# Hyena filters kept in two parts, and the side pieces of the sums over k1 placed elsewhere

## The chip, the core and the metric

The kernel runs on one core of a Trainium2 chip. TensorE (PE) multiplies matrices, its weight loads (PEld) run beside them; VectorE (DVE), ScalarE (ACT) and GpSimd (POOL) do elementwise work; SyncE (SP) issues DMAs, and so do ACT and POOL from their own instruction queues. The metric is the device time of one execution in microseconds (us), less is better. The kernel before takes 3728.32 us, the median of 3 runs (3725.71 to 3728.37).

## What is computed

One encoder block in float32. The change touches the Hyena branch alone, a gated long convolution applied twice, whose filters come from a small network over the positions:

```python
filt = (hid @ w_out).reshape(l, HYENA_ORDER, 2, HYENA_WIDTH)
filt = filt * jnp.exp(-t[:, None] * deltas[None, :])[:, None, None, :]   # decay
kern = jnp.concatenate([filt[:, :, 0], zeros, filt[:0:-1, :, 1]], axis=0)
spec = jnp.fft.rfft(kern, axis=0)                                        # L = 2048, CW = 512 channels

def long_conv(z, spec):
    zf = jnp.fft.rfft(z, n=2 * l, axis=1)
    return jnp.fft.irfft(zf * spec[None], n=2 * l, axis=1)[:, :l]

for n in range(2):                                  # the two orders
    z = gates[n] * (long_conv(z, spec[:, n]) + skip[n] * z)
```

## The kernel before

Every float32 product is made of two-part operands: `split` (L40 to L43) writes hi, a rounded copy, on ACT and lo, the rest, on DVE; `mm3` (L46 to L50) is three matmuls: hi hi, hi lo, lo hi. In the trace L42 and L43 are such splits, and L48 to L50 the three matmuls.

The stages follow each other: the projections (to about 690 us), attention (to about 1510), the Hyena branch (to about 2095), the merge (to about 2600) and the experts. All engines work through fixed queues; a scheduler sets each queue's order ahead of the run from the order of the code.

**The filters.** `filter_gen` (L629) runs as a side piece of the projections, one step beside one group of their matmuls, from about 315 to 592 us. For 4 blocks of channels, 2 orders and 4 pieces of positions it makes two tiles `fo` (128x512): two matmuls each (L654), a product with the decay `dc` on DVE (L656), and two stores of 128 KB on SP's queue (`store_l1`) into the scratch array `filt`.

**The Hyena branch.** `hyena_phase` (L669) transforms in two steps, n = n1, n2 and k = k1, k2, in four rounds: two orders, two halves of the channels. A round has three transforms forward: the two filters (`spectrum` with s = 0 and s = 1) and the data (`conv`). Each begins with `first`, the sums over n1: 8 pieces of 128x512, for each 12 matmuls of 256 columns against `d1` (so 96 in all) and two splits of the sums into `bh` (ACT) and `bl` (DVE). The sums over n2 follow, for the filters 132 matmuls of the table `tf` in 9 steps. `conv` makes its sums over n2, multiplies with the spectrum (`ya`, cut by ACT into `yh` and by POOL into `yl`) and sums back over k2 with tables `tg`, in 17 steps (`back`: ACT takes the result out as `vo` and stores it in `s_v`). `last` then sums over k1: 16 tiles `vr` are read back from `s_v`, split into `vh` and `vl`, multiplied with `d3` (6 matmuls a tile), scaled with the skip and gated (`z`, `g`).

`last` is a generator of 36 steps, and it runs as the side piece of the round that follows: `next(side)` takes a step. In the kernel before, `first` takes one at every second piece, `spectrum` 14 over its 9 steps (9, and 5 more at every k0 that divides by 4), and what is left is drained ahead of `conv`. In the first round the side piece is the rest of the gate projection (matmuls `gp` with tiles `gu`) and a step is taken at every piece.

**The pieces.** `parts_of` (L723) reads filters and data alike: SP loads a raw piece `zr` of 256 KB (L731), in 512-byte runs, up to 3 ahead; `split_pool` (L719) cuts it into `zh` on ACT (L720) and `zl` on POOL (L721).

Of the kernel before, what the change touches and what calls it, by code (L numbers as in the profile page):

```python
# [19 lines left out]
L = 2048  # L20
# [73 lines left out]
def proj_phase(E, x, norm1_g, w_in, conv_w, conv_b, qg, kg, rope, qn, kn, vs, hyc, ud, sg, mlp, gen):  # L94
# [6 lines left out]
    with ExitStack() as ctx:  # L101
# [76 lines left out]
        with pool_of(tc, name="pj_q", bufs=2) as pq:  # L178
            with pool_of(tc, name="pj_x", bufs=4) as px, pool_of(tc, name="pj_pt", bufs=3, space=PSUM) as pt:
                turn(0, px, pt)  # L180
                w = weights(0)
                gq = pc.tile([128, 2, DK], F32, name="gq")
                nc.sync.dma_start(gq[:, 0], dap(qg, 0, [[0, 128], [1, DK]]))
                nc.sync.dma_start(gq[:, 1], dap(kg, 0, [[0, 128], [1, DK]]))
                rp = pc.tile([128, NT, 2, 16], F32, name="rp")
# [443 lines left out]
def filter_gen(E, w, tabs, hsd, filt):  # L629

    nc, tc = E.nc, E.tc
    with pool_of(tc, name="fl_o", bufs=2, side="right") as po, pool_of(tc, name="fg_ps", bufs=2, space=PSUM) as ps:
        for ct in range(4):
            for o in range(2):
                wo = po.tile([128, 2, 128], F32, name="wo", bufs=1)
                for s in range(2):
                    nc.sync.dma_start(wo[s * 64:(s + 1) * 64], w["w_out"][0].rearrange("h (o s c) -> h o s c", o=2, s=2)
                                      [:, o, :, ct * 128:(ct + 1) * 128])
                weo = po.tile([128, 2, 128], F32, name="weo", bufs=1)
                nc.vector.tensor_tensor(weo[:, 0], wo[:, 0], wo[:, 1], ALU.add)  # L640
                nc.vector.tensor_tensor(weo[:, 1], wo[:, 0], wo[:, 1], ALU.subtract)
                wh = po.tile([128, 2, 128], F32R, name="woh")
                wl = po.tile([128, 2, 128], F32R, name="wol")
                split(nc, wh, wl, weo)
                for i in range(4):
                    dc = po.tile([128, 512], F32, name="dc")
                    nc.sync.dma_start(dc, tabs["decay"][ct * 128:(ct + 1) * 128, i * 512:(i + 1) * 512])
                    hs = po.tile([128, 512], F32R, name="hs")
                    nc.gpsimd.dma_start(hs, hsd[:, i * 512:(i + 1) * 512])
                    fs = []  # L650
                    for s in range(2):
                        p = ps.tile([128, 512], F32, name="fq")
                        for a, ww in enumerate((wh, wl)):
                            nc.tensor.matmul(p, ww[:, s], hs, start=a == 0, stop=a == 1)  # L654
# [3 lines left out]
                        if s == 0:  # L658
                            yield
                    if i == 0:  # L660
                        c = po.tile([128, 1], F32, name="c0")
                        nc.vector.tensor_tensor(c, fs[0][:, 0:1], fs[1][:, 0:1], ALU.add)
                        nc.vector.tensor_scalar(fs[0][:, 0:1], c, 0.5, None, ALU.mult)
                    for s in range(2):
                        store_l1(nc.sync, filt, (o * 2 + s) * CW * L, ct, i, fs[s])
                    yield


def hyena_phase(E, hyc, filt, skip, tabs, scr, hT, filler, then):  # L669
# [7 lines left out]
    with pool_of(tc, name="hy_d", bufs=1) as pd, ExitStack() as right:  # L677
        with ExitStack() as ctx:
# [21 lines left out]
            with pool_of(tc, name="hy_e", bufs=1) as pe:  # L700
                ex = pe.tile([8, 128], F32, name="ex")
                nc.sync.dma_start(ex, tabs["ex"])
                sk = pe.tile([8, 2, 64], F32, name="sk")
                for o in range(2):
                    nc.sync.dma_start(sk[:, o], dap(skip, o * CW, [[64, 8], [1, 64]]))
                skb = pd.tile([128, 2, 64], F32, name="skb")
                p = s1.tile([128, 128], F32, name="p1")
                nc.tensor.matmul(p, ex, sk.rearrange("p o g -> p (o g)"), start=True, stop=True)
                nc.scalar.activation(skb, p.rearrange("p (o g) -> p o g", o=2), AF.Copy)
# [13 lines left out]
            def parts_of(jobs):  # L723

                todo = [(src, hf * 8 + q) for src, hf in jobs for q in range(8)]
                loads, ready = [], []

                def load():
                    src, q = todo.pop(0)
                    r = p1.tile([128, 4, 128], F32, name="zr", bufs=AHEAD)  # L730
                    nc.sync.dma_start(r, dap(src, q * 512, [[8192, 128], [128, 4], [1, 128]]))  # L731
                    loads.append(r)

                def cut():
                    r = loads.pop(0)
                    zh = p1.tile([128, 4, 128], F32R, name="zh", bufs=CUT[0])
                    zl = p1.tile([128, 4, 128], F32R, name="zl", bufs=CUT[0])
                    split_pool(zh, zl, r)
                    ready.append((zh, zl))
                    if todo:  # L740
                        load()
# [3 lines left out]
                cut()  # L745
                while ready:
                    while loads and len(ready) < CUT[0]:
                        cut()
                    yield ready.pop(0)

            AHEAD, CUT = 3, [2]

            def first(it, v, side, busy=False):
# [3 lines left out]
                for q in range(8):  # L757
# [10 lines left out]
                    if busy or q % 2:  # L768
                        next(side, None)
# [969 lines left out]
```

## Time and profile before

| what | value |
| --- | --- |
| median of 3 runs | 3728.32 us (3725.71 to 3728.37) |
| profiled execution, its own time | 3731.11 us |
| its span, first to last instruction | 3729.3 us |
| mean granted TensorE clock | 0.987 |
| PE busy | 3608.1 us, 97% |
| DVE busy | 2472.5 us, 66% |
| ACT busy | 1819.2 us, 49% |
| POOL busy | 412.9 us, 11% |
| DMA | 607.28 MB, mean 163 GB/s |

Busy shares are means over stages with different limits. A stretch of the trace is read by its length, the matmuls that PE has in it, and what ended PE's waits. Matmuls of one chain overlap: the time from one start to the next, the pitch, is what a matmul costs, and it is less than its duration.

### The profile page before, as it was taken

To read this page: it belongs to the slowest core of one execution; us is meant where nothing else is said; L and a number is where in the kernel's file an instruction comes from. 1 tells how busy PE (TensorE), PEld (TensorE's weight loads), DVE (VectorE), ACT (ScalarE), POOL (GpSimd) and SP (SyncE) were. 2 spreads that over 40 slices of the span, in tenths; PEclk is the share of its full clock that TensorE was granted. 3 is DMA by queue.
4 is the path that set the end of the run, shared out by engine and by line. 5 is a ranking of instruction groups with operands and counts; after the bars stand their busy time and mean duration, and the time that the engine had idled before them with its cause. 6 is when DMAs were issued, how large, how long until landed. Compare 5 with 4: busy or idle time off the path is not lost. (4 is left out here: it accounts for less than half of the span.)

```text
span 3729.3 us, 55700 instructions
## 1 busy us (share of the span) xinstructions
PE 3608.1 (97%) x21122; PEld 3117.1 (84%) x21122; DVE 2472.5 (66%) x5459; ACT 1819.2 (49%) x2787; POOL 412.9 (11%) x423
## 2 busy tenths in 40 slices
PE   8999999999999999999999799998999999999998
PEld 6788888788888888788998678887998888888887
DVE  8944552598989898256787754548875666665663
ACT  5411111566676666357667533323445555555553
POOL 0000000000000000344553200000000101101000
PEclk9999999999999999999999899998999999999999
DMA  4286774322222231757776853324666766766664
GB/s 157 75 246 170 193 187 135 119 64 68 96 81 94 68 102 60 227 165 227 210 214 192 286 170 130 115 91 138 216 194 204 222 206 208 221 203 210 220 204 123
DMA packets 449713, 607.28 MB, mean 163 GB/s; under 512 B 37467, under 2 KB 333411, under 8 KB 442789
## 3 DMA queue, kind: packets, MB, share of 16 engines
q1 hardware_dynamic: 388149, 436.71, 37.1%
q0 software_dynamic: 34736, 127.16, 12.7%
q10 hardware_dynamic: 26560, 39.85, 3.0%
q8 instruction: 166, 2.72, 0.3%
q14 instruction: 102, 0.84, 0.1%
HBM read 464.16 MB, written 139.46 MB: 162 GB/s over the span
## 5 line engine op out<-in xcount | busy, mean ns | idle before, releaser
L43 DVE TENSOR_TENSOR wl<-r,wh 128x2048 fp32r<-128x2048 f32 (+1 forms) x248 | 476.9, 1928 | 333.1 <-ACT wh L42 333.0
L42 ACT ACTIVATE wh<-r 128x2048 fp32r<-128x2048 f32 (+1 forms) x248 | 402.5, 1624 | 383.6 <-PE pg L1616 138.4
L1616 PE MATMUL pg<-x,wh 128*128 128x512 f32 x1664 | 587.0, 398 | 0.0
L1619 PE MATMUL pg<-x,wl 128*128 128x256 f32 x1664 | 466.3, 280 | 0.0
L1616 PEld LDWEIGHTS pg<-x,wh 128*128 128x128 f32 x1664 | 312.4, 188 | 75.3
L411 DVE TENSOR_SCALAR_CACHE_REDUCE x<-p 128x512 f32<-128x512 f32 x512 | 335.0, 685 | 22.8 <-PE p L410 22.0
L410 PE MATMUL p<-k,qT 128*128 128x512 f32 x1024 | 327.3, 415 | 0.0
L1619 PEld LDWEIGHTS pg<-x,wl 128*128 128x128 f32 x1664 | 314.1, 189 | 0.5
L418 ACT ACTIVATE x<-x,sm 128x2048 f32<-128x2048 f32 x128 | 256.7, 2005 | 45.8 <-DVE sm L415 42.0
L42 ACT ACTIVATE ah<-pt 128x512 fp32r<-128x512 f32 x256 | 150.2, 595 | 151.9 <-PE pt L433 151.3
L48 PE MATMUL p<-wh,uh 128*128 128x512 f32 x512 | 203.5, 398 | 0.4 <-ACT uh L134 0.4
L49 PE MATMUL py<-wl,hh 128*128 128x512 f32 x512 | 203.3, 397 | 0.0
L48 PE MATMUL py<-wh,hh 128*128 128x512 f32 x512 | 201.8, 394 | 0.0
L43 DVE TENSOR_TENSOR bl<-p,bh 128x512 fp32r<-128x512 f32 x192 | 124.6, 685 | 115.5 <-ACT bh L42 114.7
L49 PE MATMUL p<-wl,uh 128*128 128x512 f32 x512 | 200.5, 392 | 0.4 <-DVE wl L43 0.4
L50 PE MATMUL py<-wh,hl 128*128 128x512 f32 x512 | 200.5, 392 | 0.0
L43 DVE TENSOR_TENSOR al<-pt,ah 128x512 fp32r<-128x512 f32 x256 | 174.9, 686 | 38.5 <-ACT ah L42 37.5
L50 PE MATMUL p<-wh,ul 128*128 128x512 f32 x512 | 200.4, 392 | 0.0
L410 PEld LDWEIGHTS p<-k,qT 128*128 128x128 f32 x1024 | 171.3, 189 | 24.4 <-ACT qT L368 2.8
L433 PE MATMUL pt<-idf,x 128*128 128x128 f32 x1024 | 164.7, 272 | 0.0
L48 PE MATMUL gp<-gh,gu 128*128 128x512 f32 x384 | 158.3, 412 | 4.1 <-ACT go L294 3.4
L1642 POOL DMA_INDIRECT out_dram<-y,ix x32 | 67.8, 2118 | 808.0 <-ACT y L1641 698.3
(433 smaller groups left out, 9346.8 us busy)
## 6 DMA issues: line engine op xcount, KB each, us to landing
r<-in_w_gate SPq DMA_DIRECT2D x64, 1024.0 KB, 5.2
r<-in_w_up SPq DMA_DIRECT2D x64, 1024.0 KB, 5.8
r<-in_w_down SPq DMA_DIRECT2D x64, 1024.0 KB, 5.8
gu<-s_ud POOLq DMA_DIRECT2D x48, 1024.0 KB, 5.9
tg<-in_tg POOLq DMA_DIRECT2D x68, 384.0 KB, 4.2
xt<-in_x SPq DMA_DIRECT2D x32, 512.0 KB, 4.3
s_filt<-fo SPq DMA_DIRECT2D x128, 128.0 KB, 3.2
zr<-s_filt SPq DMA_DIRECT2D x64, 256.0 KB, 3.1
```

The lines of the kernel that those rows point to most:

```text
L42: nc.scalar.activation(hi, src, AF.Copy)
L43: return nc.vector.tensor_tensor(lo, src, hi.bitcast(F32), ALU.subtract)
L48: nc.tensor.matmul(out, a[0], b[0], start=start, stop=False)
L49: nc.tensor.matmul(out, a[0], b[1], start=False, stop=False)
L50: return nc.tensor.matmul(out, a[1], b[0], start=False, stop=stop)
L410: nc.tensor.matmul(p, qT[:, t * 2 + m, a], k2[:, m, o:o + 512], start=a == 0, stop=a == 1)
L411: nc.vector.tensor_scalar(x[:, o:o + 512], p, 0.125, None, ALU.mult, ALU.max, accum_out=sm[:, c * 2 + i:c * 2 + i + 1])
L418: nc.scalar.activation(x, x, AF.Exp, bias=sm[:, 8 + m:9 + m], accum_out=acc)
L433: nc.tensor.transpose(p[:, i, t * 128:(t + 1) * 128], EX[u, t, 0][:, (g * 2 + i) * 128:(g * 2 + i + 1) * 128], E.idf)
L1616: nc.tensor.matmul(p.rearrange("p a c -> p (a c)"), wt[0][:, k, cs], x2[:, k].rearrange("p a c -> p (a c)"), start=k == 0, stop=False, ski ...
L1619: nc.tensor.matmul(p[:, 0], wt[1][:, k, cs], x2[:, k, 0], start=False, stop=k == KD - 1, skip_group_check=True)
L1642: nc.gpsimd.indirect_dma_start(out=rows, out_offset=bass.IndirectOffsetOnAxis(ap=ix[:, s:s + 1], axis=0), in_=y, in_offset=None, compute_o ...
```

## The change

`filter_gen` now cuts each tile itself: ACT writes hi and DVE writes lo, side by side in a tile of 128x4x2x128, and `keep` stores both, two DMAs of 256 KB a tile in runs of 1 KB. The scratch array is twice as large. The loops over orders and pieces change places, so that `dc` and `hs` are loaded once for both orders (16 times each, and not 32). The factors from `w_out` take the buffers of `dc`, and two small constants move between pools (left out below).

`parts_of` reads a filter piece ready cut, hi and lo in one DMA of 512 KB, now from POOL's queue, into 4 buffers; a data piece is still raw, read by SP and cut by ACT and POOL. The load of piece n + 4 is issued after piece n is used.

The side steps: `first` takes one at its sixth piece and five behind its last; `spectrum` takes 9 and one more; `conv` takes 6 in `first` and drains the rest behind it.

```diff
         for ct in range(4):
-            for o in range(2):
...
-                for i in range(4):
...
+            ww = [factors(ct, o) for o in range(2)]
+            for i in range(4):
+                dc = po.tile([128, 4, 128], F32, name="dc")
...
+                for o in range(2):
                     fs = []
                     for s in range(2):
                         p = ps.tile([128, 512], F32, name="fq")
...
-                        f = po.tile([128, 512], F32, name="fo")
-                        nc.vector.tensor_tensor(f, p, dc, ALU.mult)
+                        f = po.tile([128, 4, 2, 128], F32R, name="fo")
+                        nc.vector.tensor_tensor(f[:, :, 1].bitcast(F32), p.rearrange("p (a b) -> p a b", b=128), dc,
+                                                ALU.mult)
...
+        def keep(f, o, s, ct, i):
+            raw = f[:, :, 1].bitcast(F32)
+            split(nc, f[:, :, 0], f[:, :, 1], raw)
+            for h in range(2):
+                nc.sync.dma_start(dap(filt, (o * 2 + s) * CW * L * 2 + ((ct * 2 + h) * 16 + i * 4) * 16384,
+                                      [[256, 64], [16384, 4], [1, 256]]),
+                                  f[h * 64:(h + 1) * 64].rearrange("p a b c -> p a (b c)").bitcast(F32))
...
                 def load():
-                    src, q = todo.pop(0)
-                    r = p1.tile([128, 4, 128], F32, name="zr", bufs=AHEAD)
-                    nc.sync.dma_start(r, dap(src, q * 512, [[8192, 128], [128, 4], [1, 128]]))
-                    loads.append(r)
+                    src, q, two = todo.pop(0)
+                    z = p1.tile([128, 4, 2, 128], F32R, name="zz", bufs=AHEAD)
+                    r = None
+                    if two:
+                        nc.gpsimd.dma_start(z.rearrange("p a b c -> p (a b c)"),
+                                            dap(src, q * 1024, [[16384, 128], [1, 1024]]))
+                    else:
+                        r = px.tile([128, 4, 128], F32, name=("ya", "vo")[q % 2], bufs=2)
+                        nc.sync.dma_start(r, dap(src, q * 512, [[8192, 128], [128, 4], [1, 128]]))
+                    loads.append((z, r))
...
                         split(nc, hi, lo, p.rearrange("p g k c -> p k g c"))
-                    if busy or q % 2:
+                    if busy or q == 5:
+                        next(side, None)
+                if not busy:
+                    for _ in range(5):
                         next(side, None)
                 return B
...
-                    if not busy and k0 % 4 == 0:
+                    if not busy and k0 == 8:
                         next(side, None)
...
-                B = first(it, 0, side)
+                B = first(it, 0, side, False)
+                for _ in side:
+                    pass
...
-                    for _ in side:
-                        pass
                     conv(it, hf, side)
```

ACT's queue at the first piece sums of a later round (s = 0, the stretch from 1696.7 to 1708.0 us in the trace of before). `zh` is the cut of a piece, `bh` the first part of the sums over n1, `vh` of a tile read back for the sums over k1, `sp` the spectrum. Before:

```order
L720 ACTIVATE zh<-zr 128x512
L42 ACTIVATE vh<-vr 128x512
L42 ACTIVATE bh<-p_16965 128x32x16
L42 ACTIVATE bh<-p_16974 128x32x16
L720 ACTIVATE zh<-zr 128x512
L42 ACTIVATE bh<-p_16989 128x32x16
L42 ACTIVATE bh<-p_16998 128x32x16
L42 ACTIVATE vh<-vr 128x512
```

The same place after:

```order
L42 ACTIVATE bh<-p_16872 128x32x16
L42 ACTIVATE bh<-p_16881 128x32x16
L42 ACTIVATE vh<-vr 128x512
L42 ACTIVATE bh<-p_16898 128x32x16
L42 ACTIVATE bh<-p_16907 128x32x16
L42 ACTIVATE vh<-vr 128x512
L42 ACTIVATE bh<-p_16918 128x32x16
L42 ACTIVATE bh<-p_16927 128x32x16
L42 ACTIVATE vh<-vr 128x512
```

The cuts `zh` are gone from this place; the first `vh` still stands ahead of the last copies of the sums, four here and two before.

ACT's queue at the second filter of the same round (s = 1, 1725.1 to 1739.3 us before). `z` is the scaling with the skip. Before:

```order
L42 ACTIVATE bh<-p_17311 128x32x16
L720 ACTIVATE zh<-zr 128x512
L42 ACTIVATE bh<-p_17332 128x32x16
L42 ACTIVATE bh<-p_17341 128x32x16
L720 ACTIVATE zh<-zr 128x512
L42 ACTIVATE bh<-p_17356 128x32x16
L42 ACTIVATE bh<-p_17365 128x32x16
L720 ACTIVATE zh<-zr 128x512
L42 ACTIVATE vh<-vr 128x512
```

After, where `zz<-ya` and `zz<-vo` are cuts of the data pieces that follow:

```order
L42 ACTIVATE bh<-p_17257 128x32x16
L918 ACTIVATE z<-z,skb 128x128
L42 ACTIVATE bh<-p_17268 128x32x16
L918 ACTIVATE z<-z,skb 128x128
L42 ACTIVATE bh<-p_17277 128x32x16
L739 ACTIVATE zz<-ya 128x4x128
L42 ACTIVATE bh<-p_17289 128x32x16
L42 ACTIVATE bh<-p_17298 128x32x16
L739 ACTIVATE zz<-vo 128x4x128
```

Between two copies of the sums there stands now a cut for the data or a scaling, and no longer the cut that the next matmuls of this stretch need.

POOL's queue at the end of a round, where `conv` runs out and the next round's filter pieces come. Before:

```order
L832 DMA tg<-in_tg 128x768
L721 TENSOR_TENSOR yl<-ya,yh 128x512
L832 DMA tg<-in_tg 128x768 x2
L721 TENSOR_TENSOR yl<-ya,yh 128x512
L721 TENSOR_TENSOR zl<-zr,zh 128x512
L832 DMA tg<-in_tg 128x768
```

After:

```order
L740 TENSOR_TENSOR yl<-ya,yh 128x512
L753 DMA zz<-s_filt 128x1024
L860 DMA tg<-in_tg 128x768
L740 TENSOR_TENSOR yl<-ya,yh 128x512
L753 DMA zz<-s_filt 128x1024
L860 DMA tg<-in_tg 128x768
L753 DMA zz<-s_filt 128x1024 x5
```

Loads of filter pieces, each of which waits for PE to free its buffer, now stand in this queue ahead of the last `yl` of the round.

## Rows read from the trace of the kernel before

**Rows 1.** Waits, 1525 to 2095 us: waiting engine, line, cause: us, times, longest.

```profile
PE p L48 <- DVE bl L43: 14.0, 10, 2.3
...
PE p L50 <- POOL yl L721: 2.9, 8, 0.5
...
ACT vh L42 <- DMA vr<-s_v: 15.9, 13, 2.6
```

**Rows 2.** Windows: length, busy (count) of PE, PEld, DVE, ACT, POOL; clock, DMA share, GB/s.

```profile
1533.30:1555.50 22.20, 19.65 (x126) 16.93 (x125) 10.59 (x16) 14.18 (x26) 16.16 (x17) 1.00 0.88 277
1604.80:1615.70 10.90, 8.36 (x62) 7.35 (x60) 5.87 (x9) 8.61 (x19) 6.03 (x7) 1.00 0.97 293
1725.10:1739.30 14.20, 13.06 (x104) 12.45 (x103) 12.46 (x22) 13.35 (x29) 8.38 (x7) 1.00 0.71 220
1858.00:1872.70 14.70, 13.49 (x105) 12.60 (x104) 12.39 (x22) 13.52 (x29) 8.40 (x7) 1.00 0.77 223
1987.50:2003.90 16.40, 14.20 (x104) 13.74 (x104) 13.33 (x23) 14.06 (x30) 9.05 (x7) 0.91 0.74 227
1627.80:1641.90 14.10, 13.02 (x107) 12.61 (x105) 9.54 (x15) 12.45 (x25) 8.75 (x7) 1.00 0.34 96
...
2021.40:2035.50 14.10, 11.96 (x97) 11.55 (x96) 10.88 (x21) 11.85 (x24) 6.47 (x5) 1.00 0.38 132
1696.70:1708.00 11.30, 8.99 (x70) 8.35 (x68) 7.34 (x12) 9.46 (x19) 7.65 (x8) 0.97 0.70 215
...
1739.30:1760.50 21.20, 18.76 (x146) 17.61 (x145) 10.58 (x22) 12.65 (x31) 2.48 (x3) 1.00 0.70 228
...
2003.90:2021.40 17.50, 17.50 (x147) 17.50 (x146) 9.72 (x21) 12.84 (x30) 1.84 (x2) 0.99 0.74 239
...
1800.00:1810.00 10.00, 10.00 (x86) 10.00 (x85) 8.69 (x20) 5.53 (x12) 7.08 (x8) 1.00 0.82 215
2000.00:2010.00 10.00, 10.00 (x74) 10.00 (x73) 6.61 (x13) 8.53 (x20) 3.64 (x5) 0.83 0.83 269
...
1520.00:1530.00 10.00, 7.61 (x27) 5.83 (x26) 0.00 (x0) 0.60 (x1) 4.58 (x9) 0.83 1.12 356
540.00:560.00 20.00, 20.00 (x89) 16.47 (x88) 8.71 (x16) 2.41 (x4) 1.06 (x2) 1.00 0.66 164
```

**Rows 3.** Groups by form, 1525 to 2095 us: busy, mean ns of one, idle before.

```profile
L43 DVE TENSOR_TENSOR bl<-p,bh 128x512 fp32r<-128x512 f32 x192 | 124.6, 685 | 115.5 <-ACT bh L42 114.7
...
L720 ACT ACTIVATE zh<-zr 128x512 fp32r<-128x512 f32 x96 | 61.1, 637 | 13.2 <-DMA zr<-s_filt 8.5 <-DMA zr<-s_hyc 2.0 <-DMA zr<-s_z 1.7
```

**Rows 4.** Timeline of PE, ACT, DVE, POOL: start, us, instruction, idle before it and cause.

```profile
1706.81 0.38 PE L48 MATMUL p<-vh,d 128*128 128x256 f32 x1 [2.31 <-DVE bl L43]
...
1999.66 0.39 PE L48 MATMUL p<-d,zh 128*128 128x256 f32 x1 [2.10 <-DVE bl L43]
...
1696.89 0.60 ACT L815 ACTIVATE vo<-p 128x512 f32<-128x512 f32 x1 [0.58 <-PE p L50]
...
1704.80 0.63 ACT L42 ACTIVATE vh<-vr 128x512 fp32r<-128x512 f32 x1 [0.61 <-DMA vr<-s_v]
1705.34 1.07 ACT L42 ACTIVATE bh<-p 128x512 fp32r<-128x512 f32 x2
...
1706.07 2.66 DVE L43 TENSOR_TENSOR bl<-p,bh 128x512 fp32r<-128x512 f32 x4
...
1697.16 0.55 POOL L832 DMA_DIRECT2D tg<-in_tg  x1
```

**Rows 5.** DMA issues of the whole run: queue, count, KB each, median us to landing.

```profile
tg<-in_tg POOLq DMA_DIRECT2D x68, 384.0 KB, 4.2
xt<-in_x SPq DMA_DIRECT2D x32, 512.0 KB, 4.3
```

**Rows 6.** Tile `fo`: what DVE, idle, waited for before it: us, times.

```profile
  DMA dc<-in_decay: 10.0, 4
  DMA s_filt<-fo: 4.5, 2
```

More of the change, by code (lines that the diff above doesn't have):

```diff
@@ new lines, in factors @@
+        def factors(ct, o):
+            wo = po.tile([128, 4, 128], F32, name="dc")
+            for s in range(2):
+                nc.sync.dma_start(wo[s * 64:(s + 1) * 64, :2],
+                                  w["w_out"][0].rearrange("h (o s c) -> h o s c", o=2, s=2)
+                                  [:, o, :, ct * 128:(ct + 1) * 128])
+            nc.vector.tensor_tensor(wo[:, 2], wo[:, 0], wo[:, 1], ALU.add)
+            nc.vector.tensor_tensor(wo[:, 3], wo[:, 0], wo[:, 1], ALU.subtract)
+            wh = po.tile([128, 2, 128], F32R, name="woh")
+            wl = po.tile([128, 2, 128], F32R, name="wol")
+            split(nc, wh, wl, wo[:, 2:])
+            return wh, wl
@@ new lines, in keep @@
+        def keep(f, o, s, ct, i):
[5 more added lines that the diff above has]
+                                  f[h * 64:(h + 1) * 64].rearrange("p a b c -> p a (b c)").bitcast(F32))
+        for ct in range(4):
+            ww = [factors(ct, o) for o in range(2)]
+            for i in range(4):
+                dc = po.tile([128, 4, 128], F32, name="dc")
+                nc.sync.dma_start(dc.rearrange("p a b -> p (a b)"),
+                                  tabs["decay"][ct * 128:(ct + 1) * 128, i * 512:(i + 1) * 512])
+                hs = po.tile([128, 512], F32R, name="hs")
+                nc.gpsimd.dma_start(hs, hsd[:, i * 512:(i + 1) * 512])
+                for o in range(2):
@@ L699, in hyena_phase @@
             nc.gpsimd.dma_start(d3, tabs["d3"])
[L700 to L709, printed above, removed]
+            AHEAD = 4
+            e2 = p1.tile([8, 2, 128], F32, name="zz", bufs=AHEAD)
+            nc.sync.dma_start(e2[:, 0], tabs["ex"])
+            for o in range(2):
+                nc.sync.dma_start(e2[:, 1, o * 64:(o + 1) * 64], dap(skip, o * CW, [[64, 8], [1, 64]]))
+            skb = pd.tile([128, 2, 64], F32, name="skb")
+            p = s1.tile([128, 128], F32, name="p1")
+            nc.tensor.matmul(p, e2[:, 0], e2[:, 1], start=True, stop=True)
+            nc.scalar.activation(skb, p.rearrange("p (o g) -> p o g", o=2), AF.Copy)
             TF = {}
@@ L723, in parts_of @@
             def parts_of(jobs):
-                todo = [(src, hf * 8 + q) for src, hf in jobs for q in range(8)]
+                todo = [(src, hf * 8 + q, two) for src, hf, two in jobs for q in range(8)]
                 loads, ready = [], []
                 def load():
-                    src, q = todo.pop(0)
-                    r = p1.tile([128, 4, 128], F32, name="zr", bufs=AHEAD)
-                    nc.sync.dma_start(r, dap(src, q * 512, [[8192, 128], [128, 4], [1, 128]]))
-                    loads.append(r)
@@ L740, in cut @@
+                    loads.append((z, r))
+                def cut():
+                    z, r = loads.pop(0)
+                    if r is not None:
+                        split_pool(z[:, :, 0], z[:, :, 1], r)
+                    ready.append(z)
+                while todo and len(loads) < AHEAD:
+                    load()
+                while loads:
+                    while loads and len(ready) < 3:
+                        cut()
+                    yield ready.pop(0)
                     if todo:
@@ L741, in cut, with first @@
                         load()
-                while todo and len(loads) < AHEAD:
-                    load()
[L745 to L753, printed above, removed]
+                yield from ready
+            def first(it, v, side, busy):
                 B = (pb.tile([128, KR, 256], F32R, name="bh"), pb.tile([128, KR, 256], F32R, name="bl"))
@@ L757, in first @@
                 for q in range(8):
-                    zh, zl = next(it)
+                    z = next(it)
                     for a in range(2):
```

47 lines of the change are left out of this document (15 added, 32 removed).

## The prediction

> **What bounds the kernel now.** I read the busy shares first: PE is busy for 97% of the span, so a change pays only where PE stands still or runs slower, and of the rest nothing is worth a look unless PE waits for it. The waits of PE inside the Hyena branch come next [rows 1]: the largest is for `bl`, the second part of the sums over n1 (14.0 us in 10 waits); those for `yl` are small, 2.9 us. The first part feeds it: DVE sat idle for 115.5 us ahead of the `bl`, nearly all of it waiting for ACT's `bh` [rows 3]. So ACT sets the pace of the sums over n1.
>
> Windows of the branch by stage then give a loss for each stretch: its length less its matmuls times their pitch. PE never stands still from 1800 to 1810 us and starts 86 matmuls of 256 columns there, so the pitch is 10/86 = 0.116 us; from 540 to 560 it starts 89, mostly of 512 columns, which makes 0.225 us [rows 2]. A piece is 12 matmuls, 1.40 us of PE. For it ACT makes two `bh`, started 1.07 us a pair [rows 4], and, before the change, one `zh` of 0.64 us [rows 3]; consecutive ACT copies start about 0.1 us sooner than their durations add up to, so a piece costs ACT about 1.6 us, more than PE's 1.40, with the `vh` and `z` of the side piece on top. DVE's `bl`, four in 2.66 us [rows 4], need 1.33 us a piece: they just fit.
>
> The losses so found [rows 2]: the four sums over n1 of s = 1 lose 3.7 (10.9 us with 62 matmuls), 2.1 (14.2 with 104), 2.5 (14.7 with 105) and 4.3 (16.4 with 104), together 12.6 us. The first stretch of the branch loses 22.2 - 96 x 0.116 - 30 x 0.225 = 4.3. Those of s = 0 lose 11.3 - 70 x 0.116 = 3.2 in the one shown; two others are alike (11.5 and 11.2 us long). The four data stretches lose between 1.0 and 2.8; the first and the last are shown (1.7 and 2.8), and the sum is 6.7. The sums over n2 behind s = 1 lose 4.2 in the one from 1739.3 and 0.4 in the one from 2003.9; 1.2 lies between.
>
> There is a second loss. The window from 2000 to 2010 us has PE busy throughout, but 74 matmuls and not 86, at a granted clock of 0.83 [rows 2]; it begins with a pause of 2.10 us that ended at 1999.66 [rows 4]. The clock has two levels here, 2.4 and 1.2 GHz, and 0.83 over 10 us is 3.4 us at the lower one: 0.17 x 10 = 1.7 us lost. The pause of 2.31 us before 1706.81 [rows 4] is followed by the same.
>
> **Part by part.** Gains are negative.
>
> *First stretch, filter pieces ready cut.* ACT loses 8 `zh` and POOL 8 `zl` that PE's first 96 matmuls waited for. What can go is the loss of 4.3. What can come are waits for loads twice as large, on POOL's queue among the tables for the sums over n2, in a stretch that already moves 277 GB/s [rows 2]: 2 MB more at the highest rate shown, 356 GB/s, are 5.9 us, of which the loads issued ahead of the stretch hide some. Bounds -4.3 and +4; I take -3, near the lower, as PE's own work of 18 us leaves 2.2 us for each of the 8 loads.
>
> *Sums over n1 of s = 1.* ACT loses 8 `zh` a stretch and takes 4 cuts of the data instead, of the same 0.64 us; most of the `vh` move behind the sums. The order shows `bh` pairs with one cut or one short `z` between. That is 8 x 1.07 + 4 x 0.54 + some z and vh, about 13 us beside PE's 12.2: nearly balanced, and what is late is off PE's path, since the cuts are for the next stretch. What is late next are the loads. A piece's load is issued when the fourth before it is used, 3 x 1.40 = 4.2 us ahead of its need, and POOL's issue itself takes 0.55 [rows 4]. By size it lies between `tg` (384 KB, 4.2 us) and anything larger; `xt`, of the same 512 KB, took 4.3 us [rows 5]. So the first late piece slips by about 0.6 us, later ones by 0.1 to 0.2 each: 1.0 us a stretch, and 0.3 for the rest. The first of the four I leave 1.4 us more of its 3.7, since the tables of the first round are still being loaded beside it (293 GB/s). -12.6 + 4 x 1.3 + 1.4 = **-6.0**. Bounds: -11 if loads and copies both keep up, +7 by the first rival.
>
> A rule of the Trainium skill bears on this term and can be left out of it: the page "DMA: Bandwidth & Descriptors", section "Anatomy of one DMA — SWDGE (gpsimd) path", fits the time of a DMA from POOL's queue as 2.0 us plus its bytes over 436 thousand per us. By it `tg` would land after 2.9 us, where the trace has 4.2, so the measurement decides here; with the page's 3.2 us for 512 KB the loads would never slip, and the sum would be lower by 4 x 1.0 us.
>
> *The clock behind 2003.9.* The pause of 2.10 us is one of ACT's and goes with it: **-1.7** (0 if it stays above 2 us).
>
> *Sums over n2 of s = 1.* They took 14 side steps and take 10, with fewer copies between ACT's `sp`: of 5.8 us lost I take **-2.3**; bounds 0 and -4.5.
>
> *Data stretches.* The first four pieces are cut ahead of the stretch, during s = 1, and the side pieces stand behind the sums, where the copies of the last `bl` would have made PE wait: the `d3` matmuls fill that. Of 6.7 us **-3**; bounds 0 and -5. The loads are as large as before.
>
> *Sums over n1 of s = 0, rounds 2 to 4.* Here the end is set by another chain: the last `back` of the round before is done at 1696.89, ACT's `vo` is stored, SP reads `vr` back, and ACT's `vh` starts at 1704.80, having waited for that read [rows 4] (such waits are 15.9 us over the branch [rows 1]). The changed order keeps that `vh` in ACT's queue, now ahead of four `bh` of this stretch and not two. Behind it DVE has two `vl` and five `bl`, some 4.7 us, to do before the sums over n2 can begin; before it had one `vl` and four `bl` (3.3 us). So the stretch grows by about 1.4 us less the 0.2 that the `zh` cost: **+1.2 x 3 = +3.6**, and the pause of 2.3 us with its slower clock stays. Bounds: -6 (a read that lands by the time its turn comes leaves only PE's work) and +6.
>
> *The last `yl` of a round.* On POOL's queue it stands behind a load that waits until PE has used the first piece of the next round (12 matmuls, 1.4 us); PE's last `back` needs that `yl`. Hitherto each of these waits was 0.5 us at most [rows 1]. About 1.2 us of stall, less 0.5 that PE can fill with sums over n1 that are ready: 0.7 x 3 = **+2**; bounds 0 and +4. Behind the load queue also a `tg`, which has two steps of slack.
>
> *Projections.* 64 tiles are cut, each 0.6 us of ACT and 0.69 of DVE. Between 315 and 592 us PE does not wait for the filters: in the 20 us shown it is at 20.00 while DVE has 8.71 and ACT 2.41 [rows 2]. The two stores of a tile grow from 128 to 256 KB on SP's queue and the ring `fo` has two buffers; DVE waited 4.5 us for it and 10.0 for `dc` [rows 6], and of `dc` half the loads go. Cover is PE's queue of matmuls that need neither. **+1**; bounds 0 and +8, the latter if a late `fq` stops PE's queue at a change of weights, with four such tiles ahead of it.
>
> **Sum.** -3 - 6.0 - 1.7 - 2.3 - 3 + 3.6 + 2 + 1 = -9.4 us. The profiled execution took 3731.1 and would take 3721.7. It lies 2.8 us above the median of the three timed runs, which therefore goes from 3728.3 to **3719**.
>
> **Rivals.** *Loads become the bound (slower).* Filter pieces ask for 524 KB each 1.40 us, 375 GB/s, and the highest that the branch shows is 356 GB/s, with the DMA engines' share above 1 [rows 2]. The other traffic in the s = 1 stretch from 1987.5 is 227 GB/s x 16.4 us less 8 x 262 KB, so 99 GB/s, which leaves 257, or 2.04 us a piece. Three pieces at 0.64 and the first 0.6 make 2.5 us a stretch, over 8 stretches 20 us, of which 7.6 stand in the sum: +12.4. Pauses of that size would bring the lower clock to four stretches, +6.8: **3738**. It decides from about 2 us a stretch. Against it: much of that other traffic are reads for the side piece, which moves behind the sums, and a read of 4 KB runs asks for fewer packets than one of 512 bytes. Chance 0.15.
>
> In a sentence by itself: the Trainium skill, "Trainium Kernel Development and Optimization", section "Key Constraints", says that DMAs from SP, ACT and POOL run on the same 16 DMA engines and interleave, so that moving the filter loads to POOL's queue gives them no bandwidth of their own; no row here contradicts it.
>
> *The pauses move and stay.* The sums over n2 wait behind the side pieces for the same `bl` and `vl`; only the first stretch, the data and half of s = 1 gain: -3 - 3 - 3 + 3.6 + 2 + 1 = -2.4, **3726**, no measurable change. For it speaks that DVE needs 1.33 of 1.40 us a piece [rows 4], which five side steps add to. Chance 0.22.
>
> *More than that.* The stretch from 2021.4 loses 2.8 us in shorter pauses at a granted clock of 1.00 [rows 2]; only the pauses above 2 us have the slower clock behind them. If the five side steps behind the sums fill those, three more dips of 1.7 go, s = 0 costs nothing instead of 3.6, and the loads slip by 0.3: -5.1 - 3.6 - 2.8 = -11.5 beyond the forecast, **3707.5**. Chance 0.15.
>
> *Projections stall* at +8 instead of +1: **3726**. Chance 0.06. The forecast itself, 3712 to 3726, keeps 0.42.
>
> **Chances and range.** A measurement tells about 0.2% from no change, 7.5 us: faster is below 3720.9, slower above 3735.8. The forecast lies on that line's faster side by 2 us, so it gives 0.25 to faster and 0.17 to same; the second rival 0.04 and 0.18, the third 0.15 to faster, the first 0.15 to slower, the last 0.05 to same and 0.01 to slower. Faster 0.44, same 0.40, slower 0.16. The range runs from 3702, below the third rival's time, to 3738, the first's.
>
> **What would show it.** Right: s = 1 stretches of about 13 us with no `zh` on ACT and waits of PE for `zz` loads near 1 us; s = 0 stretches near 12.5 us ended by `vh` waiting for `vr`; PE at 10.00 in the projections' windows. Wrong: waits of PE for `zz` above 2 us a stretch (first rival), long waits for `bl` still behind s = 1 (second), a granted clock of 1.00 behind every sum over n1 (third), PE idle between 315 and 620 us (fourth).

## The result, and the profile after

The changed kernel takes 3779.37 us (median of 4 runs, 3776.23 to 3785.95) against 3728.35 us beside it: a ratio of 1.0132, with a 95% interval of 1.0119 to 1.0144. It is 51 us slower where I forecast 9 us less. Its profiled execution has a span of 3780.4 us at a mean clock of 0.983.

Two markers place the loss. The first weight load of the gate projection `gp` ends the projections, the first of the merge, `pb`, ends the Hyena branch. The rows are those of tiles `gp` and `hi`, with first and last start; before comes first, after second.

```profile
L48 PEld LDWEIGHTS gp<-gh,gu x384: 186/188/333, 687.7 to 1603.9; 128*128 128x128 f32 x192
L48 PEld LDWEIGHTS pb<-wah,hi x128: 186/188/333, 2095.1 to 2496.0; 128*128 128x128 f32 x128
```

```profile
L48 PEld LDWEIGHTS gp<-gh,gu x384: 186/188/333, 707.9 to 1625.6; 128*128 128x128 f32 x192
L48 PEld LDWEIGHTS pb<-wah,hi x128: 186/188/334, 2147.9 to 2546.3; 128*128 128x128 f32 x128
```

The projections end 20.2 us later. From there to the merge it was 1407.4 us and is 1440.0: 32.6 more. Attention lies in that stretch; up to the branch's first sums over n1 it took 845.6 us and takes 847.5. What follows the merge's start is 1.7 us shorter. So there are two losses, in two stages, of which the sum had +1 and about -10.

PE's waits in the branch, 1500 to 2150 us, answer [rows 1]: engine, line, cause, us in total, times, longest.

```profile
PE p L48 <- DVE bl L43: 21.5, 12, 4.8
PE p L48 <- DMA zz<-s_filt: 20.6, 13, 7.2
PE p L48 <- ACT vo L843: 9.3, 8, 3.8
...
PE p L50 <- POOL yl L740: 2.5, 4, 0.7
```

The waits for `bl`, which the change was to remove, grew from 14.0 to 21.5; a new one for filter pieces, 20.6 us, stands beside them. In the projections PE waited for nothing of the sort before. Now, 250 to 700 us:

```profile
PE fq L670 <- DVE fo L672: 6.0, 4, 2.3
PE p L48 <- ACT wh L42: 5.6, 3, 3.4
```

Windows of the changed kernel (columns as in [rows 2]): first the projections where the loss lies, then the three s = 0 stretches of rounds 2 to 4.

```profile
510.00:520.00 10.00, 5.33 (x13) 2.76 (x12) 5.10 (x8) 2.41 (x4) 0.53 (x1) 0.70 0.70 185
520.00:530.00 10.00, 6.93 (x26) 4.67 (x25) 3.03 (x5) 1.78 (x3) 0.00 (x0) 0.96 0.78 224
530.00:540.00 10.00, 7.83 (x23) 6.20 (x24) 7.85 (x16) 4.72 (x9) 0.53 (x1) 0.66 0.85 242
...
630.00:640.00 10.00, 8.09 (x28) 6.07 (x27) 0.92 (x3) 4.30 (x6) 2.13 (x3) 0.83 0.51 172
```

```profile
1722.40:1739.00 16.60, 10.19 (x78) 9.26 (x76) 7.79 (x12) 8.35 (x15) 4.23 (x8) 1.00 1.12 392
1860.60:1879.60 19.00, 11.53 (x80) 10.78 (x79) 8.77 (x15) 8.15 (x15) 3.92 (x8) 0.90 1.01 348
2000.20:2019.80 19.60, 12.02 (x81) 10.88 (x80) 8.87 (x15) 8.14 (x15) 4.23 (x8) 0.90 1.00 340
```

**The projections.** From 510 to 540 us PE starts 62 matmuls where 136 fit, and from 630 to 640 28 of 46: 92 matmuls of 0.225 us, 20.7 us, the whole loss. The waits named there are some 11.6 us; the granted clock of 0.66 and 0.70 shows the rest, PE at the lower level after pauses of 2.2 to 3.4 us. Both places are boundaries between blocks of weights. SP's queue around the first, with start, time and instruction:

```profile
515.49 4.65 SPq L653 DMA_DIRECT2D s_filt<-fo  x4
520.18 0.80 SPq L143 DMA_DIRECT2D r<-in_w_in  x1
521.81 5.32 SPq L653 DMA_DIRECT2D s_filt<-fo  x4
527.18 0.79 SPq L143 DMA_DIRECT2D r<-in_w_in  x1
```

The next block's weights `r` stand between groups of four filter stores, and each group waits until its tiles are cut. PE meanwhile waits for the products and then for the weights:

```profile
514.08 0.79 PE L670 MATMUL fq<-hs,woh 128*128 128x512 f32 x1 [2.31 <-DVE fo L672]
...
532.17 0.80 PE L48 MATMUL p<-uh,wh 128*128 128x512 f32 x1 [3.42 <-ACT wh L42]
```

**The branch.** From the first matmul over n1 behind the last `back` to the first over n2, the s = 0 stretches of rounds 2 to 4 grew from 11.3, 11.5 and 11.2 us to 16.7, 19.0 and 19.6: 21.3 us of the 32.6. In them PE now waits 7.0 us for pieces, where it waited for none, and 14.5 us for `bl`, where it was 6.9. The DMA engines were busy for 0.70 to 0.80 there at 215 to 245 GB/s, and now for all the time at 340 to 392. Round 3 on ACT, SP and PE:

```profile
1862.05 0.60 ACT L843 ACTIVATE vo<-p 128x512 f32<-128x512 f32 x1 [1.96 <-DMA s_v<-vo]
1862.68 0.37 ACTq L848 DMA_DIRECT2D s_v<-vo  x1
...
1874.89 0.63 ACT L42 ACTIVATE vh<-vr 128x512 fp32r<-128x512 f32 x1 [6.29 <-DMA vr<-s_v]
```

```profile
1869.62 0.88 SPq L894 DMA_DIRECT2D vr<-s_v  x2
```

```profile
1876.90 0.58 PE L48 MATMUL p<-d,zz 128*128 128x256 f32 x1 [4.81 <-DVE bl L43]
```

The chain that ended this stretch before still ends it, and it is longer: `vo` to `vh` took 7.9 us [rows 4] and takes 12.8 (13.3 in round 2, 16.3 in round 4). The store in `s_v` alone needs 6.9 us until SP may read it back (4.4 before). ACT stands at that `vh` for 6.29 us with copies of the sums behind it, DVE gets no `bl`, PE's four PSUM buffers fill, and it waits for 4.81 us. Earlier in the same stretch it waits for pieces.

The pieces land late, by the page of the changed kernel:

```profile
s_filt<-fo SPq DMA_DIRECT2D x128, 256.0 KB, 3.7
zz<-s_filt POOLq DMA_DIRECT2D x64, 512.0 KB, 5.9
```

And in the first round the last piece stands in POOL's queue behind two tables that wait for room which PE frees:

```profile
1629.38 1.06 POOL L860 DMA_DIRECT2D tg<-in_tg  x2 [4.60 <-PE p L50]
1630.42 0.55 POOL L753 DMA_DIRECT2D zz<-s_filt  x1
```

```profile
1639.71 0.55 PE L48 MATMUL p<-d,zz 128*128 128x256 f32 x1 [7.23 <-DMA zz<-s_filt]
```

Once issued, that piece took 9.2 us to land.

### The profile page after: what moved, and what is told of

Same layout as the page of the kernel before. It is cut to its first block, busy times and chain, and to the rows that moved or that the text cites. A ratio compares the mean times of both kernels' runs of the same rounds, so it can differ in the third digit from the quotient of the medians.

```text
span 3780.4 us, 55603 instructions
## 1 busy us (share of the span) xinstructions
PE 3618.6 (96%) x21122; PEld 3124.6 (83%) x21122; DVE 2512.6 (66%) x5523; ACT 1826.3 (48%) x2787; POOL 355.9 (9%) x407
## 2 busy tenths in 40 slices
DMA packets 445105, 632.44 MB, mean 167 GB/s; under 512 B 36955, under 2 KB 332899, under 8 KB 438181
## 5 line engine op out<-in xcount | busy, mean ns | idle before, releaser
L48 PE MATMUL p<-uh,wh 128*128 128x512 f32 x384 | 151.4, 394 | 3.9 <-ACT wh L42 3.9
```

What stands on the lines that cost most here:

```text
L48: nc.tensor.matmul(out, a[0], b[0], start=start, stop=False)
```

## Experiments

Each run is read at the two markers. "Projections" is the shift of the first `gp` against before's 687.7 us, "branch" the change of the 1407.4 us from there to `pb`; both are of single profiled executions. Kernels with the same code in the branch differ there by several us: the changed kernel +32.6, e4 +26.8 and e6 +25.9; e5 +18.3 and e9 +9.3. So only differences above some 9 us are read.

| run | projections | branch | ratio to before, interval |
| --- | --- | --- | --- |
| changed kernel | +20.2 | +32.6 | 1.0132 (1.0119 to 1.0144) |
| e1 storage alone | +17.3 | +19.8 | 1.0116 (1.0099 to 1.0132) |
| e2 side steps alone | 0.0 | +3.7 | 1.0018 (1.0008 to 1.0028) |
| e3 half pieces | +17.9 | +11.2 | 1.0080 (1.0064 to 1.0097) |
| e4 three tiles, one hs | +40.1 | +26.8 | 1.0202 (1.0185 to 1.0219) |
| e5 two queues exchanged | +20.8 | +18.3 | 1.0109 (1.0092 to 1.0126) |
| e6 no subtraction | +22.8 | +25.9 | 1.0169 (1.0152 to 1.0186) |
| e7 side steps alone, late | +0.4 | +5.0 | 1.0014 (1.0005 to 1.0024) |
| e8 three tiles; half pieces, SP | +37.4 | +5.0 | 1.0111 (1.0094 to 1.0128) |
| e9 four PSUM; SP | +18.8 | +9.3 | 1.0098 (1.0078 to 1.0118) |
| e10 before, added traffic | +43.9 | +0.5 | 1.0124 (1.0103 to 1.0145) |
| e11 before, added copies | +1.2 | -3.4 | 1.0001 (0.9988 to 1.0014) |
| e12 storage, both queues, four PSUM | +13.7 | +10.6 | 1.0069 (1.0050 to 1.0088) |
| e13 before, stores from POOL; burst | +13.6 | +10.7 | 1.0068 (1.0051 to 1.0085) |
| e14 before, other stores on SP; lead of two | +41.4 | +18.0 | 1.0154 (1.0137 to 1.0171) |

**Which half of the change.** e1 is the changed kernel with the old places of the side steps (and the rest drained ahead of the data again), e2 the kernel before with the new ones; e1's edit:

```diff
-                    if busy or q == 5:
+                    if busy or q % 2:
...
-                    if not busy and k0 == 8:
+                    if not busy and k0 % 4 == 0:
```

> The changed kernel with the side steps where they were before (every second piece, 14 in the sums over n2, the rest drained ahead of the data): the storage part alone. Theory A (the doubled filter loads saturate the DMA engines and delay the chain s_v, vr, vh in the s = 0 stretches; the projections lose 20 us by themselves): the projections keep their +20, the Hyena branch loses 15 to 30 against before, so 3763 to 3780. Rival B (the branch loses by the new places of the side steps): the branch is back to its old length, 3748.

> The kernel before with only the side steps moved as in the change; filters stored and read as before. Theory A: no loss in the projections and none in the branch, 3720 to 3732. Rival B: the branch loses most of its 30 us here too, 3745 to 3758.

Storage alone costs 37 us in the two stages, the side steps alone 3.7; e2's 1.0018 excludes a gain. So the loss is storage's, theory A's side. Together they cost in the branch 26 to 33, more than the sum of 23.5 or about as much, by the spread above. e7 puts all six side steps behind the sums and none among them:

```diff
-                    if busy or q == 5:
+                    if busy:
...
-                    for _ in range(5):
+                    for _ in range(6):
```

> The kernel before with the side steps of the change, except that none is taken among the sums over n1: all six stand behind them. Filters stored and read as before. If vh among the copies of the sums cost the s = 0 stretches their time, this is 3 to 8 us faster than the side steps of the change alone: 3724 to 3732. If the pause only moves, 3734 to 3738.

It is no better than e2 (+5.0 and +3.7). In e2 the s = 0 stretches are a little shorter than before (10.3, 10.5 and 10.6 us), but the drained steps lengthen the data stretches: from the first sum over n1 to the first over n2 they take 15.9, 16.8 and 15.2 us in rounds 2 to 4, against 13.5, 13.3 and 14.1 before (15.2, 17.2 and 16.4 in e7). The pause moves and stays, as the second rival had it.

**The bytes of the pieces.** e3 reads half of each piece and multiplies it twice:

```diff
-                        nc.gpsimd.dma_start(z.rearrange("p a b c -> p (a b c)"),
-                                            dap(src, q * 1024, [[16384, 128], [1, 1024]]))
+                        nc.gpsimd.dma_start(z[:, :2].rearrange("p a b c -> p (a b c)"),
+                                            dap(src, q * 1024, [[16384, 128], [1, 512]]))
```

> The changed kernel with filter pieces of which only half is read (256 KB in runs of 2 KB, and each half is multiplied twice), so the filters' lower half is left out of the computation; all matmuls, copies and side steps stay. Theory A: the waits for filter pieces and the long waits for vr go, the branch gains 20 to 30 us, 3750 to 3760, with the projections' +20 left. Rival B: 3770 to 3780.

The branch falls from +32.6 to +11.2, the projections keep theirs, and the s = 0 stretches are 11.8, 13.7 and 13.8 us. A piece now lands, in the median, in

```profile
zz<-s_filt POOLq DMA_DIRECT2D x64, 256.0 KB, 4.1
```

That is inside the 4.2 us of lead, and 5.9 was not.

**The queue of the pieces.** e5 loads them from SP's queue and stores the filters from POOL's:

```diff
-                        nc.gpsimd.dma_start(z.rearrange("p a b c -> p (a b c)"),
+                        nc.sync.dma_start(z.rearrange("p a b c -> p (a b c)").bitcast(F32),
...
-                nc.sync.dma_start(dap(filt, (o * 2 + s) * CW * L * 2
+                nc.gpsimd.dma_start(dap(filt, (o * 2 + s) * CW * L * 2
```

> The changed kernel with two queues exchanged: the filter pieces of the branch are loaded from SP's queue (as before) and the filter stores of the projections issued from POOL's. The stages are separate, so each tells of its own. Projections: if SP's queue, where the loads of weights stand behind stores that wait for their tile, is the cause, PE's waits for wh go and most of the 20 us; if the ring of two tiles alone is, PE's waits for fo stay and 10 us or more are left. Branch: if the queue is a cause beside the bytes, the wait of 7 us in the first round and the waits for yl go, 8 to 12 us, and the pieces still come late; if only the bytes count, the branch keeps its +33.

The branch falls to +18.3, the pause of 7.23 us in the first round becomes one of 3.71, the waits for `yl` stay (2.7 us), the pieces still land after 6.1 us and PE still waits 20.4 us for them. In the projections PE's waits for `wh` shrink to 1.4 us, yet the stage keeps its +20.8: other waits, for `fo` (4.9), `wl` (3.2) and `woh` (2.3), took their place. The expectation that one of queue and ring would show alone fell.

**Ring, copies, PSUM in the projections.** e4 gives the tiles a third buffer and takes one from `hs` and one from the raw weights; e6 leaves out the subtraction:

```diff
-            split(nc, f[:, :, 0], f[:, :, 1], raw)
+            nc.scalar.activation(f[:, :, 0], raw, AF.Copy)
```

> The changed kernel with three buffers for the cut filter tiles instead of two (hs gets one and the raw weights three, to make room). Theory A': the projections' 20 us come from the ring of two buffers, each of which is away for the cut and both stores: with three most of it goes, 3760 to 3768. Rival B': it is SP's queue, in which stores stand ahead of the loads of weights, or the added copies themselves: 3775 to 3785.

> The changed kernel without the subtraction that makes the lower part of the filters (DVE, 0.69 us a tile), which is left out of the computation; copy, stores and bytes stay. If the time in which a tile is away (product, copy, subtraction, two stores) sets the projections, this shortens it by about 0.75 of 7 to 8 us and the projections gain 3 to 10 of their 20 us; if it is the stores' queue alone, 0 to 3. The branch stays.

e4 tells nothing of the ring: PE now waits for `hs` (17.2 us) and `wh` (10.0), the buffers that I took. In e6 the tile is away for less and the stage is no shorter. e8 takes the room from the raw weights alone (two instead of four), and joins e3's half pieces with SP's queue; e9 doubles the PSUM buffers `fq` and loads the pieces from SP:

```diff
-                        f = po.tile([128, 4, 2, 128], F32R, name="fo")
+                        f = po.tile([128, 4, 2, 128], F32R, name="fo", bufs=3)
...
-    ... pool_of(tc, name="fg_ps", bufs=2, space=PSUM) as ps:
+    ... pool_of(tc, name="fg_ps", bufs=4, space=PSUM) as ps:
```

> Two separate stages changed in the changed kernel. Projections: three buffers for the cut tiles and two for the raw weights (for room), all else as it was. If the ring of two tiles sets PE's waits, its waits for fo go and 8 to 20 of the 20 us return; if not, the waits for fo or for weights stay near 12 us. Branch: filter pieces of which only half is read (the rest is left out of the computation), from SP's queue. If bytes and queue are all that the storage costs there, the branch is within 5 us of the kernel before with the moved side steps alone (1411 us from the first gate matmul to the merge); if the placement costs more once pieces come cut, it stays 8 us or more above.

> The changed kernel with four PSUM buffers for the filter products instead of two, and the filter pieces loaded from SP's queue. Projections: if PE loses its time because bunches of products run ahead of the two tiles, four sums in PSUM take up a bunch and 8 to 15 of the 20 us return; if the weights are late behind the stores on SP's queue, at most 5 return and PE's waits for wh stay. Branch: as with both queues exchanged, 13 to 16 us less than the changed kernel.

e8 in the projections: the ring's waits of DVE fall from 25.0 to 8.3 us, but DVE now waits 34.6 us for late weights, and PE's `fq` stand behind that (9.2), its `wh` for 11.2. e9 changes little there; its branch falls by 23.3 us, where 13 to 16 were expected. In the branch of e8, half the bytes on SP's queue leave +5.0, no more than the side steps alone: within the spread of these runs, bytes and queue are all that storage costs.

**The suspects added to the kernel before.** e11 cuts each filter tile into a spare one and stores as before; e10 stores each tile twice, the second time to a spare array:

```diff
                     for s in range(2):
                         store_l1(nc.sync, filt, (o * 2 + s) * CW * L, ct, i, fs[s])
+                        store_l1(nc.sync, E.spare, (o * 2 + s) * CW * L, ct, i, fs[s])
```

> The kernel before with the cut of the change added in the projections alone: ACT and DVE cut each filter tile into a spare tile that is not stored; stores as before. If the added copies set the projections' loss: 8 to 20 us; if stores and ring do: under 4 us.

> The kernel before with traffic added and nothing else. Branch, rounds 2 to 4: beside each load of a filter piece a copy of 256 KB between two spare arrays in memory, from the same queue, that nothing waits for: the bytes of the change without its changed order. Theory A (bytes): the s = 0 stretches grow by 3 to 8 us each by late vr and late pieces, 10 to 25 us in all. Rival (queue order and the changed copies): under 5 us. Projections: each filter tile is stored twice, the second time to a spare array: the store bytes and SP's doubled issues without the copies. If stores and the ring set the projections: 8 to 25 us; if the copies on ACT and DVE do: under 4 us.

The copies cost 1.2 us, the stores 43.9: not the work on ACT and DVE, but the stores. (e10 issues twice as many stores as the change, so 43.9 is not the change's size.) The branch part of e10 tested nothing, since its copies between spare arrays, on which nothing waits, were put early in SP's queue and ran before 700 us:

```profile
L735 SPq DMA_DIRECT2D s_dump<-s_spare x48: 469/591/1410, 606.7 to 699.3; - x48
```

By then PE's long pauses were over: from 600 to 725 us it waited 1.3 us in all.

e13 and e14 were to part the two ways in which a store hurts. e13 makes the second stores from POOL's queue, so that a tile is away longer and SP is free of them; e14 stores the decay tile `dc` from SP's queue, so that SP has the issues and the tiles are not away longer:

```diff
+                        store_l1(nc.gpsimd, E.spare, (o * 2 + s) * CW * L, ct, i, fs[s])
```

```diff
+                        store_l1(nc.sync, E.spare, (o * 2 + s) * CW * L, ct, i, dc)
```

> The kernel before. Projections: each filter tile is stored a second time, to a spare array, from POOL's queue, so that the tile is away longer and SP's queue is as before. If the time in which a tile is away sets the loss, 10 to 30 us; if it is SP's queue, under 4. Branch: at the start of the s = 0 stretches of rounds 2 to 4, 8 writes of 256 KB of an old spectrum tile to a spare array. If contention alone delays s_v and vr, these stretches grow from 11.3 to 14 us or more, 8 to 20 us in all; if the pieces' own lateness sets them, under 4.

> The kernel before. Projections: the decay tile dc is stored to a spare array, four stores of 128 KB beside each four of the filters, from SP's queue: the issues and bytes of the doubled stores, while the filter tiles are away no longer than before. If SP's queue with the weights behind the stores sets the loss, 8 to 25 us; if the ring does, under 4. Branch: filter and data pieces are loaded two ahead instead of three in rounds 2 to 4. If late pieces set the loss, 6 to 20 us; if their lead does not matter, under 3.

e13 costs 13.6 us, e14 41.4. The cleanest pair are e10 and e13, the same second stores from SP's queue and from POOL's: 43.9 and 13.6. PE's waits from 250 to 690 us, all of 1 us or more, first in e13, then in e14 (left out: `fq` for `woh`, 1.7):

```profile
PE p L48 <- ACT wh L42: 8.2, 2, 4.3
```

```profile
PE p L48 <- ACT wh L42: 15.7, 3, 9.7
PE fq L654 <- DVE fo L656: 12.4, 5, 8.1
```

So the longer absence, too, reaches PE as late weights. e14 is less clean than it was meant to be: `dc` has two buffers itself, and its stores hold them. DVE's product behind the wait of 8.1 us began at 516.77, 4.0 us after a load of `dc` was issued, and these loads land in 3.4 us in the median; so SP's order and the buffers of `dc` may both be in the 41.4. And no run has the change's order of loops, or its factors in the buffers of `dc`, without its stores: what they cost by themselves in the projections is not shown.

For the branch e13 writes 2 MB of an old spectrum tile at the start of each s = 0 stretch of rounds 2 to 4, with no change to the pieces, and e14 loads pieces two ahead instead of three.

```diff
+                if s == 0 and not busy:
+                    for n in range(8):
+                        nc.sync.dma_start(E.dump[n], SP[8].rearrange("p n a b -> p (n a b)"))
```

e13's windows of rounds 2 and 3 (the s = 0 stretches) and its row of ACT:

```profile
1712.50:1727.90 15.40, 11.03 (x70) 10.26 (x69) 8.28 (x13) 10.30 (x20) 7.21 (x8) 0.79 0.89 304
1845.00:1860.10 15.10, 10.72 (x70) 10.18 (x69) 7.74 (x13) 10.00 (x20) 7.14 (x8) 0.82 0.89 298
```

```profile
1856.36 0.63 ACT L42 ACTIVATE vh<-vr 128x512 fp32r<-128x512 f32 x1 [0.45 <-DMA vr<-s_v]
```

Traffic alone lengthens the three stretches by 3.5 to 4 us each, and the chain with them: `vo` began at 1845.17, `vh` 11.2 us later (7.9 before, 12.8 in the changed kernel). But it is not the chain that PE waits for in e13. `vh` stood 0.45 us for `vr`; ACT had stood ten times as long for a raw piece, and behind that PE has its one long pause (rounds 2 and 4 are alike):

```profile
1853.78 0.63 ACT L721 ACTIVATE zh<-zr 128x512 fp32r<-128x512 f32 x1 [4.47 <-DMA zr<-s_filt]
```

```profile
1855.67 0.58 PE L48 MATMUL p<-d,zh 128*128 128x256 f32 x1 [4.38 <-DVE bl L43]
```

So e13 shows that traffic makes both the pieces and the chain late, and does not part them; that the chain holds ACT in the changed kernel is read from its own row, 6.29 us at `vh`. The writes also hold SP's queue, in which the raw pieces stand, for 6.8 us, so this is contention with some of the queue in it. The shorter lead costs 18.0 us, little of it in the s = 0 stretches (12.4, 10.8 and 11.7 us): most falls on the data's sums over n1, 14.1, 13.5, 13.3 and 14.1 us before and 16.4, 15.8, 16.3 and 17.2 now. Late pieces and a late chain are two costs; by its waits the changed kernel has both.

**Together.** e12 is storage with the old side steps, the filter stores from POOL, four PSUM buffers, pieces from SP.

> The changed kernel with the side steps of before, the filter stores on POOL's queue, four PSUM buffers for the filter products and the filter pieces loaded from SP's queue. Projections: with neither the weights behind the stores nor PE ahead of the ring, under 10 us of the 20 are left; if the ring sets the rate throughout, 12 or more. Branch: the storage's +20 falls to 5 to 15 with SP's queue if queue order counted, or stays at 20.

It is the best of the kernels with stored parts, at 1.0069, and still slower than before: +13.7 in the projections, about as much as e13, and +10.6 in the branch. In the projections PE again waits for weights alone (`wl` 6.7 us, `wh` 3.9), though no filter store stands in SP's queue. No variant beats the kernel before; e11 equals it.

## Why the prediction was wrong

**Projections: +1, bounds 0 and +8; measured +20.2.** The step that failed was the cover. I argued from a window in which PE was at 20.00 of 20 and DVE at 8.71, an average of engine time, and e11 bears that part out: the copies cost 1.2 us. What I priced at nothing was the order in which SP issues. I wrote that the stores grow on SP's queue, and did not list what stands behind them there: the weights of the next block, the one thing at a boundary that PE has no cover for. A store now becomes ready 1.4 us later (a copy and a subtraction), in a ring of two, and the weights wait with it. The place I named for the bound, a change of weights with four tiles ahead, was right; the 8 us were too few: the waits alone are 11.6 us, and behind them PE ran at the lower of its two levels, 1.2 GHz (granted clock 0.70, 0.96, 0.66 and 0.83 in the four windows), which is 8.5 us more. How the 20 us part between ring and queue inside the changed kernel stays open: e10 and e13 show that added stores cost PE time from either queue (43.9 and 13.6 us), and no run that lifts one of the two (e5, e8, e9, e12) gets more than 6.5 us back.

**Sums over n1 of s = 1: -6.0; measured +8.8** (from the first sum over n1 to the first over n2, the four stretches took 26.6, 15.3, 15.8 and 17.6 us and take 32.4, 17.2, 16.7 and 17.8). The gain from the removed cuts on ACT was real: with pieces of half the size from SP's queue (e8) those of rounds 2 to 4 take 13.6, 13.7 and 14.1 us, 7.2 less than before. The whole pieces took its place. The mis-sized term is the load: I took 4.3 us from `xt` [rows 5], a load of the same size in a stage with less traffic, and it was 5.9 (3.8 to 9.9). Against a lead of 4.2 us that is 1.7 late and not 0.1. (POOL's 0.55 us for an issue, which I added for the first piece, is part of a load's time already.) The first rival's arithmetic, engines that are full, does not fit these stretches, where the DMA engines' share is 0.69 to 0.73; it fits those of s = 0. The 7.23 us of the first round, POOL's order of tables and pieces and a piece that took 9.2 us to land, I had in my sum only as 1.4.

The Trainium skill's fit (page "DMA: Bandwidth & Descriptors", section "Anatomy of one DMA — SWDGE (gpsimd) path") gives an estimate of 3.2 us for it; the shortest of the 64 took 3.8, so the trace does not agree with it beside this traffic.

**Sums over n1 of s = 0: +3.6; measured +21.3.** The mechanism was the right one: `vr` sets the end, with `vh` ahead of four copies. The size failed because I took the chain's 7.9 us as fixed and had no wait for pieces in these stretches (7.0 us). The chain has two DMAs in it, and I had just put twice the bytes beside them. e13 shows 11.2 us for it under added traffic, e3 stretches of 11.8 to 13.8 with half the bytes. Some 32 matmuls of the side piece that now stand in the three stretches are another 3.7 us.

**Data: -3; measured +5.1 over rounds 2 to 4** (13.5, 13.3 and 14.1 us became 15.1, 16.0 and 14.9)**, -1.7 in the first.** The stretches hold 12 `d3` matmuls now, 1.4 us each, and wait for `bl` (1.31, 2.51 and 1.35 us). e2 has the same stretches long without stored parts, so this is the side steps' doing.

**First stretch -3, clock -1.7, sums over n2 -2.3:** none came in the end. The first stretch (1555.4 to 1571.4 us, 96 matmuls of 256 columns and 8 of 512) loses 3.1 us by the prediction's own working, 1.2 less than before; but the way to it is 1.9 us longer, with a pause of 2.45 us right in front of it. The sums over n2 changed by 0.1 us in all over rounds 2 to 4 (20.1, 17.1 and 16.2 became 17.6, 16.9 and 19.0). The slower clock stayed in its stretch, now behind a pause of 1.96 us for a piece (0.90 from 2036.1 to 2053.9 us), and stands in others, at 0.90 in two of the windows above. My mark for it, a pause above 2 us, does not hold in the changed kernel: behind 1.69 us before 632.71 the clock fell, behind 2.51 us before 1935.19 it stayed at 1.00. **The last `yl`, +2:** waits for `yl` are 2.5 us against 2.9, so it cost nothing.

**The rivals.** The first, loads as the bound, with the lower clock behind its pauses, happened in the s = 0 stretches, at 0.15 and with 3738; the fourth, the projections, happened too. I had given each its own time and none for both. They have one root, twice the bytes through queues that others share, so their chances should have been joined: 3719 with +12.4, +6.8 and the fourth's +7 is 3745, nearer than any number I gave, and above my range. One of my arguments against the first was misread: a raw piece was not read in runs of 512 bytes but of 2 KB, as its four runs lie side by side (packets under 2 KB fell by only 512 over the whole run, from 333411 to 332899), so runs of 4 KB saved little.

## What to carry to other kernels

Before moving work from engines into bytes, list for every DMA that grows what stands behind it in its queue and which short chains of DMAs run beside it; a queue with slack on average can hold the one load that PE needs next. A load's time is to be taken from a stretch with the traffic that it will meet, and compared with its lead in matmuls, not with its bandwidth. Rivals that share a cause belong in one case with their prices added.

## What the runs showed of the hardware

The queue in which a store stands can cost more than its bytes: 128 second stores of the filter tiles, 128 KB each, cost 43.9 us from SP's queue (e10) and 13.6 from POOL's (e13). As many stores of the decay tile from SP's queue, landing in 2.8 us each, cost 41.4 (e14), in which that tile's two buffers may have a part. And a DMA of 512 KB took 5.9 us in the median from POOL's queue and 6.1 from SP's (e5), so the queue changed what stood behind it but not the time of the transfer itself.
